# A hybrid decoder layer on one core: the order in which kept weight parts and output-projection operands are made, and which halves are scaled

## The chip, the core and the metric

The kernel runs on one core of a Trainium2 chip. A core has a matrix engine (TensorE, here PE, with its weight loads as PEld), a vector engine (VectorE, DVE), an activation engine (ScalarE, ACT), a general engine (GpSimd, POOL), a queue that here issues all DMAs (SyncE, SP), an on-chip memory, and PSUM banks into which PE writes. The metric is the device time of one execution in microseconds (us), lower is better.

## What is computed

One layer over 2048 tokens of width 1024, in fp32. The part that matters here, cut from the reference:

```python
u = rmsnorm(h, attn_pre_norm[i])
proj = u @ w_in[i]
hq, hf, hi, hg, sq, sk, sv = jnp.split(proj, splits, axis=-1)
o_hg = hgrn2_mix(hq, hf, hi, lb_all[i])
o_hg = rmsnorm(o_hg.astype(x.dtype), hg_out_norm[i]) * jax.nn.silu(hg)
o_sb = stick_breaking_mix(...)
o_sb = rmsnorm(o_sb, sb_out_norm[i])
mix = jnp.concatenate([o_hg, o_sb], axis=-1) @ w_out[i]
h = h + rmsnorm(mix, attn_post_norm[i])
u = rmsnorm(h, ffn_pre_norm[i])
gate, up = jnp.split(u @ w_gate_up[i], [D_FF], axis=-1)
y = (jax.nn.silu(gate) * up) @ w_down[i]
h = h + rmsnorm(y, ffn_post_norm[i])
h = h + (p[i] @ ple_proj[i]) * jax.nn.sigmoid(h @ ple_gate[i])
```

`rmsnorm` divides a row by the root of its mean square plus 1e-6 and multiplies by a gain.

## The kernel before

The 2048 tokens are four groups of 512 (`NG` groups, tiles of 128x512 throughout). Every fp32 product is made of three matmuls on rounded halves: an operand is cast to a high part by ACT, a low part is the difference, made by DVE or POOL (`split`, L203 to L207), and `mm3` (L218 to L221) multiplies high by high, high by low and low by high.

The first part of the program is a plan of input projections (`in_proj`): step by step a projection's matmuls are woven with units of attention, with steps of the HGRN recurrence (`hgrn`, 46 steps a group) and with other streams. `weave` (L51) runs a main stream slot by slot and gives each other stream its share of steps; `Rate` spreads a number of steps over a number of slots. Then come two plain output projections (groups 0 and 1, `out_proj`), with the rest of attention and HGRN woven in, and one joint output projection of groups 2 and 3 (`out_pair`). Joint projections, the FFN and the last gate use a seven-product scheme (`CHAIN = (1, 2, 6, 3, 7, 5, 4)`) instead of eight block products, whose operands are sums and differences of blocks. For the output projection and two blocks of the FFN, the weight operands of some products are made early, in spare time, split, and put away in DRAM: these are the kept parts. `out_combos` (L731) and `gate_up_combos` (L706) make them, `keep` (L700) casts, subtracts and stores one; `wo_p`, `wg_p` hold them.

What sets the order: PE runs in the order of the program text. On all other engines a planner reorders instructions by a simulated timeline: what is ready may go ahead of earlier text. `tc.keep_in_program_order` pins an instruction behind the instruction that was traced last before it on its engine; later instructions are not tied to it. All DMAs are issued by SP. A tile of a pool waits until one of the pool's buffers is free; the pool `xt` has 8 buffers and serves the kept parts, the operands of the output projections (`out_load`, L629) and the token tiles; the pool `u` holds 16 pairs of split operands.

Stages by the weight casts of L205 in an answer of the trace (24 to an attention-side projection, 32 to an HGRN-side one; the last two of the plan hold 2 and 4 of `out_load`):

| stretch, us | plan step | beside it |
| --- | --- | --- |
| 89 to 192 | 0, group 1, attention side | attention |
| 192 to 333 | 1, group 0, HGRN side | attention |
| 333 to 457 | 2, group 2, attention side | `out_combos` in the text |
| 457 to 626 | 3, group 1, HGRN side | attention, HGRN |
| 626 to 786 | 4, group 3, attention side | first half of `gate_up_combos` in the text |
| 786 to 963 | 5, group 2, HGRN side | its second half in the text |
| 963 to 1158 | 6, group 3, HGRN side | `out_load(0)` at once at its start |
| 1158 to 1256 | plain output projection 0 | `out_load(1)` at once at its start |
| 1256 to 1357 | plain output projection 1 | `first_rows`, `post_mix` of group 0 |

In the output projections the two halves of a row, HGRN and attention, have each their own mean square. In the plain ones the result of each half is scaled after the product. In the joint one, where blocks of both halves are added, each half was scaled before: `over_rows` (L769) spreads the factors of 512 rows over 128 partitions by four transposes on PE, and `scaled` (L779) multiplies; group 2 in `first_rows`, group 3 in the hook `before` (L852) at the second of the chain's 28 steps. The scaled tiles of group 2 go to DRAM (`on_s`) and are loaded again by `out_pair`. `post_mix` (L905) normalises a plain projection's result, adds the residual, transposes it and writes `h_s` and `u_s`; for group 1 its transposes are evicted (L930) into the pool `acc` of two buffers.

## Time and profile before

| | us |
| --- | --- |
| median of 3 runs | 3000.83 (2997.11 to 3003.03) |
| the profiled execution's own time | 2994.58 |
| its span, first to last instruction | 2992.7 |
| PE busy in it | 2869.8 |
| DVE busy | 2113.8 |
| ACT busy | 1579.3 |
| POOL busy | 1400.4 |

Busy time of one engine can be set beside the span: what is left is idle time of that engine. In a row of a table by stretches the columns are the stretch, its length, the busy time and number of instructions of PE, PEld, DVE, ACT and POOL, the share of the full clock that PE was granted, the busy share of the DMA engines and what they moved in GB/s. A group of instructions has its line, engine, operation, the tiles out<-in, shapes and count, then busy time in us, mean ns of one, idle time of the engine before them and what ended it. A wait's row has who waited, for what, then the us in total, the number of waits and the longest one. L1050, L1051, L1063 and L1066 are lines of helpers (`pair_of`, `sub`, `add`) that many callers share.

### The profile page before, as it was taken

Reading aid. Unit: us, or ns where it says so; the run is one execution under the profiler, and the core shown is the slowest. Engines: PE = TensorE matmul, PEld = TensorE weight load, DVE = VectorE, ACT = ScalarE, POOL = GpSimd, SP = SyncE. Lnnn points to the kernel's source line nnn. Section 1 sums busy time; section 2 is a strip of 40 time slices with the busy share of each in tenths; the row PEclk is TensorE's granted clock in tenths of the full one; section 3 lists DMA queues with packets and bytes.
Section 4 is the critical chain, followed back from the end, with each engine's and each line's share of the span. In section 5 each row is a group of like instructions: output and inputs, shape, how many; then the busy total and the mean of one; then the engine's idle time right before and its main releaser. Section 6 shows DMA issues by size and latency. Waiting matters only on the chain. (4 is left out here: it accounts for less than half of the span.)

```text
span 2992.7 us, 52029 instructions
## 1 busy us (share of the span) xinstructions
PE 2869.8 (96%) x17804; PEld 2402.7 (80%) x17804; DVE 2113.8 (71%) x3055; ACT 1579.3 (53%) x3222; POOL 1400.4 (47%) x1388
## 2 busy tenths in 40 slices
PE   8999999988999998988999999999999999999999
PEld 7888778877888787877787778788888888878777
DVE  4766776778777777667876777856777766666685
ACT  5676657666666666665633333455533333545542
POOL 3345446545555667665523222355822121456653
PEclk9999999999999999999999999999999999999999
DMA  7775685468545545358896687877975555667975
GB/s 226 234 200 164 208 278 169 142 197 262 166 144 150 145 131 163 110 161 297 310 304 210 225 292 259 267 216 221 311 238 172 176 169 176 214 213 233 332 251 169
DMA packets 488137, 636.32 MB, mean 213 GB/s; under 512 B 45248, under 2 KB 275648, under 8 KB 487872
## 3 DMA queue, kind: packets, MB, share of 16 engines
q1 hardware_dynamic: 487872, 633.00, 67.3%
q8 instruction: 141, 2.31, 0.3%
q14 instruction: 124, 1.02, 0.1%
HBM read 459.29 MB, written 173.54 MB: 211 GB/s over the span
## 5 line engine op out<-in xcount | busy, mean ns | idle before, releaser
L1050 ACT CAST wh<-wr 128x512 fp32r<-128x512 f32 x592 | 346.9, 618 | 498.0 <-PE mm L220 111.1
L1051 POOL TENSOR_TENSOR wl<-wr,wh 128x512 fp32r<-128x512 f32 x256 | 369.0, 1449 | 432.4 <-ACT wh L1050 383.9
L450 POOL TENSOR_TENSOR a<-be,ring 128x512 f32<-128x512 f32 (+2 forms) x320 | 328.1, 1025 | 425.3 <-DVE ring L446 387.1
L219 PE MATMUL mm<-uh,wh 128*128 128x512 f32 x968 | 403.7, 417 | 13.1 <-DVE eb L349 5.5
L1051 DVE TENSOR_TENSOR wl<-wr,wh 128x512 fp32r<-128x512 f32 x336 | 303.6, 911 | 158.5 <-ACT wh L1050 139.6
L220 PE MATMUL mm<-ul,wh 128*128 128x512 f32 x968 | 382.5, 395 | 0.0
L221 PE MATMUL mm<-uh,wl 128*128 128x512 f32 x968 | 382.5, 395 | 0.0
L446 DVE TENSOR_TENSOR_SCAN ring<-z,ring,be 128x512 f32<-128x512 f32 x192 | 245.5, 1279 | 101.1 <-ACT z L432 93.5
L219 PE MATMUL mm<-wh,uh 128*128 128x256 f32 (+1 forms) x840 | 260.8, 310 | 1.4 <-DVE eb L349 1.3
L220 PE MATMUL mm<-wl,uh 128*128 128x256 f32 (+1 forms) x840 | 247.2, 294 | 1.6 <-POOL wl L1051 1.6
L221 PE MATMUL mm<-wh,ul 128*128 128x256 f32 (+1 forms) x840 | 246.8, 294 | 0.0
L431 ACT ACTIVATE be<-z 128x512 f32<-128x512 f32 (+2 forms) x320 | 171.1, 535 | 100.9 <-DVE z L429 57.1
L219 PEld LDWEIGHTS mm<-uh,wh 128*128 128x128 f32 x968 | 184.9, 191 | 49.0 <-DVE eb L349 5.6
L463 DVE TENSOR_TENSOR al<-tr,ah 128x512 fp32r<-128x512 f32 (+1 forms) x320 | 191.2, 598 | 44.9 <-ACT ah L461 43.2
L221 PEld LDWEIGHTS mm<-uh,wl 128*128 128x128 f32 x968 | 183.9, 190 | 41.7
L205 ACT CAST wh<-wr 128x512 fp32r<-128x512 f32 x256 | 158.5, 619 | 106.6 <-PE mm L220 53.2
L461 ACT CAST ah<-tr 128x512 fp32r<-128x512 f32 (+1 forms) x320 | 167.7, 524 | 86.7 <-PE tr L458 85.0
L220 PEld LDWEIGHTS mm<-ul,wh 128*128 128x128 f32 x968 | 184.6, 191 | 30.8
L206 POOL TENSOR_TENSOR wl<-wr,wh 128x512 fp32r<-128x512 f32 x128 | 168.9, 1319 | 85.6 <-ACT wh L205 71.5
L458 PE MATMUL tr<-ident,a 128*128 128x128 f32 x1088 | 177.3, 275 | 25.6 <-POOL a L450 22.5
L1051 POOL TENSOR_TENSOR wl<-s,wh 128x512 fp32r<-128x512 f32 x40 | 65.7, 1644 | 268.1 <-ACT wh L1050 224.3
L425 PE MATMUL z<-kt,q 128*128 128x512 f32 (+3 forms) x640 | 189.0, 376 | 0.0
(387 smaller groups left out, 7616.3 us busy)
## 6 DMA issues: line engine op xcount, KB each, us to landing
wr<-in_w_gate_up_dram SPq DMA_DIRECT2D x292, 256.0 KB, 4.3
wr<-in_w_in_dram SPq DMA_DIRECT2D x224, 256.0 KB, 3.3
wr<-hid_s SPq DMA_DIRECT2D x154, 256.0 KB, 3.4
wr<-in_w_down_dram SPq DMA_DIRECT2D x110, 256.0 KB, 3.7
wr<-h_s SPq DMA_DIRECT2D x96, 256.0 KB, 4.6
wr<-wd_s SPq DMA_DIRECT2D x88, 256.0 KB, 3.2
kt<-k_s SPq DMA_DIRECT2D x80, 256.0 KB, 3.1
vt<-v_s SPq DMA_DIRECT2D x80, 256.0 KB, 3.2
```

Of the source, the lines that this page charges most:

```text
L206: (lo_engine or nc.gpsimd).tensor_tensor(lo, src, hi.bitcast(F32), op=ALU.subtract)
L219: nc.tensor.matmul(o, l[0], r[0], start=start, stop=False)
L220: nc.tensor.matmul(o, l[0], r[1], start=False, stop=False)
L221: nc.tensor.matmul(o, l[1], r[0], start=False, stop=stop)
L425: nc.tensor.matmul(z[:, :n], st["q"][i][:, tb * P:(tb + 1) * P], ch["k"][:, :n], start=i == 0, stop=i == 1)
L431: nc.scalar.activation(be[:, :n], z[:, :n], AF.Sigmoid, scale=0.125)
L446: nc.vector.tensor_tensor_scan(r[:, o:o + n][:, ::-1], z[:, :n][:, ::-1], be[:, :n][:, ::-1], init, op0=ALU.mult, op1=ALU.bypass)
L450: nc.gpsimd.tensor_tensor(a[:, :n], be[:, :n], r[:, o + 1:o + n + 1], op=ALU.mult)
L458: nc.tensor.transpose(tr[:, tb * P:(tb + 1) * P], ch["a"][tb][:, sb * P:(sb + 1) * P], ident)
L463: nc.vector.tensor_tensor(lo[:, lo_c:], tr[:, lo_c:], hi[:, lo_c:].bitcast(F32), op=ALU.subtract)
L1050: nc.scalar.copy(hi, src)
L1051: lo_engine.tensor_tensor(lo, src, hi.bitcast(F32), op=ALU.subtract)
```

## The change

- `split` takes a function for its cast; `out_load` yields after each operand and its casts are pinned. It runs as a stream: for group 0 along plan step 6, for group 1 along the first plain output projection.
- `keep`'s subtraction and the sums and differences of `gate_up_combos` and `out_combos` are pinned, with a yield after each. `out_combos` runs along plan steps 0 and 2 (14 steps each), `gate_up_combos` along 4 and 5 (16 each). Same operations, same data.
- In the joint projection only the attention halves are scaled, by the ratio of the two halves' factors (`ratio`); the HGRN halves are used as they are, and their factor is applied with the row scales after the product. `on_s` holds the attention half alone; the HGRN blocks are loaded from `o_s`. Subtractions of HGRN blocks move ahead of the chain, the hook moves from step 1 to step 3.
- In the plain projections attention's steps go into 24 slots instead of 27, HGRN's into 27 instead of 30; the streams of `first_rows` and `post_mix` are placed anew.
- HGRN's row sums use a bank of `tr` instead of `hg`, and the evictions of group 1's `post_mix` go to the pool `wr` (12 buffers) instead of `acc`.

```diff
@@ -121,7 +121,7 @@
     hid_s = [dram.tile([DFF // 256, 7, P, GT], F32, tag=f"hid_s{i}", name=f"hid_s{i}") for i in range(2)]
-    on_s = scratch("on_s", (ND, P, GT))
+    on_s = dram.tile([HH, P, GT], F32, tag="on_s", name="on_s")
     wo_s = [dram.tile([2, P, GT], F32, tag=f"wo_s{k}", name=f"wo_s{k}") for k in range(ND // 2)]
@@ -200,9 +200,11 @@
-    def split(pool, tag, bufs, src, lo_engine=None):
+    pin = tc.keep_in_program_order
+
+    def split(pool, tag, bufs, src, lo_engine=None, placed=lambda ins: ins):
         hi, lo = operand(pool, tag, bufs)
-        nc.scalar.copy(hi, src)
+        placed(nc.scalar.copy(hi, src))
         (lo_engine or nc.gpsimd).tensor_tensor(lo, src, hi.bitcast(F32), op=ALU.subtract)
@@ -627,26 +629,25 @@
     def out_load(g, res):
-        ops = []
-        acc = None
+        ops = res["o"] = []
         for i in range(ND):
...
                 gs = g_sb[:, i - HH:i - HH + 1]
-                nc.scalar.activation(hi, raw, AF.Copy, scale=gs)
+                pin(nc.scalar.activation(hi, raw, AF.Copy, scale=gs))
                 nc.vector.scalar_tensor_tensor(lo, raw, gs, hi.bitcast(F32), op0=ALU.mult, op1=ALU.subtract)
...
                 if i == HH:
-                    acc = ev(name="oss")
-                    nc.scalar.activation(acc, raw, AF.Square)
+                    res["oss"] = ev(name="oss")
+                    nc.scalar.activation(res["oss"], raw, AF.Square)
                 else:
                     nc.scalar.activation(raw, raw, AF.Square)
-                    nc.gpsimd.tensor_tensor(acc, acc, raw, op=ALU.add)
+                    nc.gpsimd.tensor_tensor(res["oss"], res["oss"], raw, op=ALU.add)
             else:
-                ops.append(split(wpool, "u", UB, raw))
-        res["o"], res["oss"] = ops, acc
+                ops.append(split(wpool, "u", UB, raw, placed=pin))
+            yield
@@ -699,7 +700,7 @@
         nc.scalar.copy(hi.bitcast(F32R), t)
-        nc.vector.tensor_tensor(lo.bitcast(F32R), t, hi, op=ALU.subtract)
+        pin(nc.vector.tensor_tensor(lo.bitcast(F32R), t, hi, op=ALU.subtract))
         for n, e in enumerate((hi, lo)):
@@ -716,16 +717,21 @@
                 a11, a12, a21, a22 = ts
-                add(V, a22, a21, a22)
-                sub(V, a21, a11, a21)
-                sub(V, a11, a22, a11)
-                sub(V, a12, a12, a11)
+                pin(add(V, a22, a21, a22))
+                yield
+                keep(wg_p[fb][n], 5, a22)
+                yield
+                pin(sub(V, a21, a11, a21))
+                yield
+                keep(wg_p[fb][n], 7, a21)
+                yield
+                pin(sub(V, a11, a22, a11))
                 yield
                 keep(wg_p[fb][n], 6, a11)
+                yield
+                pin(sub(V, a12, a12, a11))
+                yield
                 keep(wg_p[fb][n], 3, a12)
-                yield
-                keep(wg_p[fb][n], 7, a21)
-                keep(wg_p[fb][n], 5, a22)
                 yield
@@ -734,14 +740,22 @@
                 nc.sync.dma_start(t, w_out[r:r + P, n % 2 * GT:(n % 2 + 1) * GT])
-            keep(wo_p[k], 3, ts[3])
-            yield
-            b_combos(*ts, V)
-            nc.sync.dma_start(wo_s[k][0], ts[0])
-            nc.sync.dma_start(wo_s[k][1], ts[2])
-            keep(wo_p[k], 7, ts[1])
-            yield
-            keep(wo_p[k], 6, ts[3])
+            b11, b12, b21, b22 = ts
+            keep(wo_p[k], 3, b22)
+            yield
+            pin(sub(V, b11, b12, b11))
+            nc.sync.dma_start(wo_s[k][0], b11)
+            yield
+            pin(sub(V, b12, b22, b12))
+            yield
+            keep(wo_p[k], 7, b12)
+            yield
+            pin(sub(V, b22, b22, b11))
+            yield
+            keep(wo_p[k], 6, b22)
+            yield
+            pin(sub(V, b21, b22, b21))
+            nc.sync.dma_start(wo_s[k][1], b21)
             yield
@@ -762,10 +776,15 @@
-    def row_scale(rr):
-        nc.gpsimd.tensor_scalar(rr, rr, 1.0 / (HH * P), EPS, op0=ALU.mult, op1=ALU.add)
-        nc.gpsimd.tensor_tensor(rr, rr, neghalf.to_broadcast((P, TT)), op=ALU.pow)
-        return rr
+    def ratio(g, ss):
+        x = hgss[:, g, :]
+        for t in (x, ss):
+            nc.gpsimd.tensor_scalar(t, t, 1.0 / (HH * P), EPS, op0=ALU.mult, op1=ALU.add)
+        nc.gpsimd.tensor_tensor(ss, ss, neghalf.to_broadcast((P, TT)), op=ALU.pow)
+        nc.gpsimd.tensor_tensor(ss, ss, x, op=ALU.mult)
+        nc.gpsimd.tensor_tensor(x, x, neghalf.to_broadcast((P, TT)), op=ALU.pow)
+        nc.gpsimd.tensor_tensor(ss, ss, x, op=ALU.mult)
+        return ss
@@ -775,31 +794,31 @@
-    def scaled(g, i, raw, r):
-        if i < HH:
-            (nc.gpsimd if g == NG - 1 else nc.vector).tensor_tensor(raw, raw, r, op=ALU.mult)
-        else:
-            nc.vector.scalar_tensor_tensor(raw, raw, g_sb[:, i - HH:i - HH + 1], r, op0=ALU.mult, op1=ALU.mult)
-        if g == NG - 2:
-            nc.sync.dma_start(on_s[g][i], raw)
+    def scaled(k, raw, r):
+        nc.vector.scalar_tensor_tensor(raw, raw, g_sb[:, k:k + 1], r, op0=ALU.mult, op1=ALU.mult)
...
         yield
-        ss = tile_sums(acc)
-        rr = row_scale(hgss[:, g, :]), row_scale(ss)
+        r = ratio(g, tile_sums(acc))
         yield
-        for part in range(2):
-            r = over_rows(rr[part], "tr", xt)
-            yield
-            for k in range(HH):
-                raw = xt("raw")
-                nc.sync.dma_start(raw, o_s[g][part * HH + k])
-                scaled(g, part * HH + k, raw, r)
-                tt[1 + part, k] = split(wpool, "u", UB, raw, V if k % 2 else G)
-                if k % 2:
-                    yield
+        for k in range(HH):
+            raw = xt("raw")
+            nc.sync.dma_start(raw, o_s[g][k])
+            tt[1, k] = split(wpool, "u", UB, raw, V if k % 2 else G)
+            if k % 2:
+                yield
+        r = over_rows(r, "tr", xt)
+        yield
+        for k in range(HH):
+            raw = xt("raw")
+            nc.sync.dma_start(raw, o_s[g][HH + k])
+            scaled(k, raw, r)
+            nc.sync.dma_start(on_s[k], raw)
+            tt[2, k] = split(wpool, "u", UB, raw, V if k % 2 else G)
+            if k % 2:
+                yield
@@ -829,11 +848,11 @@
             if prod == 3:
-                a12 = load(on_s[g][HH + k])
+                a12 = load(on_s[k])
                 sub(V, s2[k], a12, s2[k])
...
             elif prod == 7:
-                t = load(on_s[g][k])
+                t = load(o_s[g][k])
                 sub(V, t, t, raws[k])
@@ -850,17 +869,12 @@
         def before(pos, i):
-            if (pos, i) == (0, 1):
-                raws["r"] = [over_rows(r, "tr", new_acc) for r in rr]
+            if (pos, i) == (0, 3):
+                r = over_rows(rr, "tr", new_acc)
                 for k in range(HH):
-                    scaled(g + 1, k, raws[k], raws["r"][0])
-                for k in range(HH):
-                    scaled(g + 1, HH + k, raws[HH + k], raws["r"][1])
-                    t = load(on_s[g][k])
-                    sub(V, t, raws[k], t)
-                    add(V, t, t, raws[HH + k])
-                    s2[k] = t
-                    tt[6, k] = split(wpool, "u", UB, t, V)
+                    scaled(k, raws[HH + k], r)
+                    add(V, s2[k], s2[k], raws[HH + k])
+                    tt[6, k] = split(wpool, "u", UB, s2[k], V)
@@ -874,6 +888,9 @@
             nc.sync.dma_start(raws[i], o_s[g + 1][i])
+        for k in range(HH):
+            s2[k] = load(o_s[g][k])
+            sub(V, s2[k], raws[k], s2[k])
         for k in range(HH):
@@ -898,8 +915,14 @@
                 half = 0 if prod == 5 else 1
-                for t in range(TT):
-                    row_rstd(None, rows_m[half][t], sums_m[half][:, 2 * t:2 * t + 2])
+                r, x = row_scales[:, half, 0:TT], hgss[:, g + half, :]
+                pair = sums_m[half].rearrange("p (t j) -> p t j", j=2)
+                nc.gpsimd.tensor_tensor(r, pair[:, :, 0], pair[:, :, 1], op=ALU.add)
+                for _ in range(2):
+                    nc.gpsimd.tensor_tensor(r, r, x, op=ALU.mult)
+                nc.gpsimd.tensor_scalar(r, r, EPS, None, op0=ALU.add)
+                nc.gpsimd.tensor_tensor(r, r, neghalf.to_broadcast((P, TT)), op=ALU.pow)
+                nc.gpsimd.tensor_tensor(r, r, x, op=ALU.mult)
@@ -1471,6 +1494,7 @@
     kept_out, kept_ffn = Stream(out_combos()), Stream(gate_up_combos())
+    loads = [Stream(out_load(g, res[g])) for g in range(2)]
     spent = 11
@@ -1484,14 +1508,14 @@
         toks = in_norm(nxt) if nxt else []
-        if n == 6:
-            out_load(0, res[0])
-        more = {2: kept_out, 4: kept_ffn, 5: kept_ffn}.get(n)
-        steps = {2: 3 * HH, 4: 6, 5: 6}.get(n)
-        more = Rate(more or idle, 1, steps or 0, slots - tail)
+        more, steps = {
+            0: (kept_out, 14), 2: (kept_out, 14), 4: (kept_ffn, 16), 5: (kept_ffn, 16), 6: (loads[0], ND)}.get(n, (idle, 0))
+        more = Rate(more, 1, steps, slots - tail)
         for r, c in zip(ra, cuts):
...
             weave(main, c, r.part(c), rh.part(c, 1 if hg_n < slots else None), more.part(c, 1))
+        if n in (2, 5, 6):
+            more.stream.drain()
         if n in (3, 5):
@@ -1501,9 +1525,9 @@
     todo = total_units - spent + LAG + 2
-    rates = Rate(att_stream, 2, todo, 2 * OP_SLOTS - 5)
+    rates = Rate(att_stream, 2, todo, 2 * OP_SLOTS - 8)
     r2 = Rate(hgs[2], 1, HG_STEPS - 42, 2)
-    r3 = Rate(hgs[3], 1, HG_STEPS, 2 * OP_SLOTS - 2)
+    r3 = Rate(hgs[3], 1, HG_STEPS, 2 * OP_SLOTS - 5)
     half = OP_SLOTS // 2
@@ -1517,22 +1541,25 @@
         if g == 0:
-            out_load(1, res[1])
             weave(op, 2, rates.part(2), r2.part(2))
             hgs[2].drain()
-            weave(op, OP_SLOTS - 2, rates.part(OP_SLOTS - 2), r3.part(OP_SLOTS - 2))
+            weave(op, OP_SLOTS - 2, rates.part(OP_SLOTS - 2), r3.part(OP_SLOTS - 2), (loads[1], ND, 0))
+            loads[1].drain()
         else:
             rows = Stream(first_rows(2, tto))
-            weave(op, 4, rates.part(4), r3.part(4), (pm, TT, 0), (rows, 2, 1))
+            weave(op, 4, rates.part(4), r3.part(4), (pm, TT, 0), (rows, 3, 1))
             weave(op, 2, rates.part(2), r3.part(2))
...
             square_sums(acc3, 0, 3, range(HH - 1), xt)
-            weave(op, 7, rates.part(7), r3.part(7), (pm, 2 * TT, 0), (rows, 5, 1))
+            weave(op, 2, rates.part(2), r3.part(2), (pm, TT // 2, 0))
             att_stream.drain()
             square_sums(acc3, 0, 3, (HH - 1,), xt)
-            weave(op, 3, r3.part(3), (rows, 2, 1))
+            weave(op, 3, r3.part(3), (pm, TT, 0), (rows, 1, 1))
+            ss3 = tile_sums(acc3)
+            weave(op, 2, r3.part(2), (pm, TT // 2, 0), (rows, 1, 1))
             hgs[3].drain()
-            rr3 = [row_scale(hgss[:, 3, :]), row_scale(tile_sums(acc3))]
+            rr3 = ratio(3, ss3)
+            weave(op, 3, (rows, 2, 1))
             rows.drain()
@@ -1544,7 +1571,7 @@
     op = Stream(out_pair(2, tto, rr3))
-    pm = Stream(post_mix(1, res[1]["mix"], ["tr", "hg", "tr"], lambda: slot("acc", 0, "acc")))
+    pm = Stream(post_mix(1, res[1]["mix"], ["tr", "hg", "tr"], lambda: slot("wr", 0, "wr")))
     def third_operands():
...
```

More of the change, by code (lines that the diff above doesn't have):

```diff
@@ L618, in hgrn @@
         yield
-        b = bank("hg")
+        b = bank("tr")
         for c in range(TT):
@@ L1062, in sub @@
     def sub(e, o, a, b):
-        e.tensor_tensor(o, a, b, op=ALU.subtract)
+        return e.tensor_tensor(o, a, b, op=ALU.subtract)
     def add(e, o, a, b):
-        e.tensor_tensor(o, a, b, op=ALU.add)
+        return e.tensor_tensor(o, a, b, op=ALU.add)
     V, G = nc.vector, nc.gpsimd
```

## The prediction

> **What bounds the kernel now.** I read the page first, then one table of busy times by stretches, cut where the changed work runs, then the waits inside those stretches.
>
> ```profile
> span 2992.7 us, 52029 instructions
> PE 2869.8 (96%) x17804; PEld 2402.7 (80%) x17804; DVE 2113.8 (71%) x3055; ACT 1579.3 (53%) x3222; POOL 1400.4 (47%) x1388
> ```
>
> TensorE (PE) is the bound. It lacks 2992.7 - 2869.8 = 122.9 us of being busy throughout, so a change that leaves its matmuls alone can win only from these idle times and from stretches in which its clock is not granted in full. The question is how much of both lies where this change works.
>
> ```profile
> core 0: us, PE busy (x) PEld busy (x) DVE busy (x) ACT busy (x) POOL busy (x), PEclk, DMA share, GB/s
> 91.00:190.00 99.00, 96.60 (x575) 83.67 (x574) 70.04 (x128) 63.90 (x143) 39.42 (x42) 1.00 0.77 220
> ...
> 336.00:424.00 88.00, 77.12 (x669) 63.52 (x667) 69.23 (x108) 49.08 (x99) 38.55 (x44) 0.94 0.85 274
> 424.00:629.00 205.00, 204.48 (x1732) 174.49 (x1731) 144.55 (x225) 143.34 (x316) 117.06 (x152) 1.00 0.58 168
> 629.00:724.00 95.00, 77.30 (x595) 61.98 (x594) 81.10 (x116) 59.49 (x122) 41.83 (x44) 0.93 0.76 235
> 724.00:788.00 64.00, 61.78 (x551) 51.76 (x551) 48.26 (x75) 42.27 (x96) 39.09 (x49) 1.00 0.66 204
> 788.00:960.00 172.00, 170.75 (x1403) 145.35 (x1403) 131.17 (x188) 117.82 (x247) 97.56 (x125) 1.00 0.50 149
> 960.00:1000.00 40.00, 35.78 (x331) 28.71 (x330) 32.03 (x43) 28.46 (x58) 30.75 (x30) 1.00 0.54 161
> 1000.00:1160.00 160.00, 155.84 (x1536) 130.41 (x1535) 116.92 (x178) 108.97 (x232) 99.76 (x122) 1.00 0.49 141
> 1160.00:1200.00 40.00, 33.73 (x323) 29.68 (x322) 26.35 (x39) 26.26 (x53) 29.76 (x38) 1.00 0.53 161
> 1200.00:1297.00 97.00, 88.46 (x1067) 80.17 (x1066) 66.08 (x110) 59.02 (x135) 65.49 (x80) 0.95 0.42 127
> 1297.00:1377.00 80.00, 66.30 (x736) 61.25 (x735) 46.25 (x77) 50.06 (x126) 47.55 (x54) 0.98 0.62 197
> 1377.00:1442.00 65.00, 54.70 (x243) 44.54 (x242) 55.50 (x77) 42.82 (x104) 31.91 (x25) 0.92 0.85 299
> 1442.00:2993.00 1551.00, 1521.62 (x6756) 1250.83 (x6754) 1088.40 (x1463) 633.83 (x1179) 615.59 (x454) 0.99 0.73 236
> ```
>
> Idle is a row's length minus its PE busy time. It is 10.9 us in 336:424 and 17.7 in 629:724, but only 0.5 in the 205 us between them and 1.3 in 788:960. The granted clock dips in the same two rows: (1 - 0.94) x 88 = 5.3 us and (1 - 0.93) x 95 = 6.7 us of full clock are missing, partly while PE idled anyway. What runs there and nowhere else is the making of kept weight parts:
>
> ```profile
> L702 DVE TENSOR_TENSOR kl<-wg,kh x16: 658/680/1578, 646.0 to 718.5; 128x512 fp32r<-128x512 f32 x16
> L702 DVE TENSOR_TENSOR kl<-wo,kh x12: 660/678/1582, 350.5 to 418.0; 128x512 fp32r<-128x512 f32 x12
> ```
>
> The program traces these over a whole input projection (`out_combos`) or two (`gate_up_combos`), but the planner lets them float forward: all 28 ran in two bursts of some 70 us. The waits (us in total, times, longest) name the link. In 336:424 PE's longest wait is for an eviction on VectorE (DVE):
>
> ```profile
> PE mm L219 <- DVE eb L349: 6.8, 3, 5.5
> ```
>
> In 629:724 it is for an attention weight of POOL, and POOL itself waited there for the scan on DVE:
>
> ```profile
> PE tr L458 <- POOL a L450: 12.5, 5, 4.7
> ```
>
> ```profile
> POOL a L450 <- DVE ring L446: 29.9, 16, 6.5
> ```
>
> Evictions and scans are DVE work, queued among the burst's.
>
> **The change part by part.**
>
> *Kept parts.* The DVE work that is moved, in 336:424
>
> ```profile
> L1063 DVE TENSOR_TENSOR wo<-wo 128x512 f32<-128x512 f32 x16 | 13.9, 869 | 5.8 <-DMA wo<-in_w_out_dram 3.8 <-issue 2.0
> L702 DVE TENSOR_TENSOR kl<-wo,kh 128x512 fp32r<-128x512 f32 x12 | 9.6, 800 | 0.4 <-DMA wo_s<-wo 0.4
> ```
>
> and in 629:724
>
> ```profile
> L702 DVE TENSOR_TENSOR kl<-wg,kh 128x512 fp32r<-128x512 f32 x16 | 14.0, 887 | 1.2 <-DMA wg_p<-kh 1.2
> L1063 DVE TENSOR_TENSOR wg<-wg 128x512 f32<-128x512 f32 x12 | 9.7, 811 | 0.0
> L1066 DVE TENSOR_TENSOR wg<-wg 128x512 f32<-128x512 f32 x4 | 3.6, 903 | 3.5 <-DMA wg<-in_w_gate_up_dram 3.4
> ```
>
> That is 13.9 + 9.6 = 23.5 us of DVE in 88 us, and 14.0 + 9.7 + 3.6 = 27.3 us in 95. A pin puts each behind the DVE instruction traced before it, so it cannot float forward. Half of the first work goes to 91:190, the rest stays in 336:460; the second spreads over 629:960. Nothing is saved on DVE; the density falls from about 27% of DVE's time to 8 to 12%. What stays of the idle (late next in the first stretch is PE itself, in the second the scan's own chain) I take from the nearest row without a burst, 724:788: 2.2 / 64 = 0.035 us per us. First stretch: 10.9 - 3 = 7.9 us won; second: 17.7 - 3.3 = 14.4. Of the clock I count two thirds: 3.5 + 4.4. Together 30.2. Bounds: at most 28.6 + 12 = 40.6, at least nothing. Where the work lands it costs something: DVE is busy 70.04 / 99 = 71% in 91:190 and 76% in 788:960. I charge 6 us, between nothing (those rows idle 2.4 and 1.3 us) and 22 (all of the excess idle moves along). The casts of the parts move along on ScalarE (ACT), one of some 0.6 us for each `kl`, 17 us in all on an engine that is 53% busy; they are not pinned. The DMAs move along on SP: 24 of the first set's 48 transfers of 128x512 fp32 enter 91:190, 6.3 MB or 64 GB/s on 220, little more than the 274 that 336:424 carried, and below the rate of 1377:1442. Net 24.
>
> A rule speaks against the spreading. The Trainium skill, "SBUF — State Buffer", section "SBUF: two separate sides", says that a DVE operation with two SBUF inputs and a GpSimd operation that reads SBUF exclude each other for a whole instruction. The trace agrees: the same subtraction took 658 ns at least and 1578 at most. By the rule 788:960, where POOL is busy 97.56 / 172 = 57% instead of 44%, makes moved operations dearer: 32 x 13% x 0.92 us, an estimated 4 us of DVE at most, and the sum would be 35 were all of that PE's.
>
> *Operand loads, `out_load`.* The same happens to the eight operands of each plain output projection:
>
> ```profile
> L634 SPq DMA_DIRECT2D raw<-o_s x16: 319/420/893, 722.7 to 990.6; - x16
> L638 ACT ACTIVATE uh<-raw,g_sb x8: 710/723/742, 970.7 to 1174.7; 128x512 fp32r<-128x512 f32 x8
> ```
>
> They are cast right at the start of the stage whose finished operands free the buffers, near 960 and 1160. Those two 40 us rows idle 4.2 and 6.3 us, against 4.2 in the 160 us between. Spread, they would keep 1 each; I take half of the rest, 4, and charge 1: 3 us. Bounds 0 and 8.
>
> *Plain output projections, 1200:1377.* Attention's steps go into 24 slots instead of 27, HGRN's into 27 instead of 30. Same work, denser early, none in the last three slots. Waits of 1160:1377:
>
> ```profile
> PE hg L604 <- DVE sl L600: 11.2, 5, 4.8
> PE hg L540 <- POOL qp L577: 8.6, 4, 3.2
> ```
>
> These belong to HGRN's own chain (mask level, POOL product, next level) and remain. The attention squares, with their loads and sums, no longer come last. I take a gain of 2; bounds: 14 gained (half of 8.5 + 13.7 idle and 6.5 clock), 19 lost (rival 2).
>
> *Joint projection, 1377:1442.* Idle 10.3, clock (1 - 0.92) x 65 = 5.2. PE's waits, then one of SP's queue, then what kept POOL:
>
> ```profile
> PE tr L926 <- ACT acc L930: 5.5, 1, 5.5
> PE z L220 <- DMA ul<-wo_p: 4.0, 1, 4.0
> ```
>
> ```profile
> SPq L917 <- POOL h L916: 5.1, 1, 5.1
> ```
>
> ```profile
> 1392.22 2.68 SPq L917 DMA_DIRECT2D h_s<-h  x2
> 1394.99 1.35 SPq L818 DMA_DIRECT2D uh<-wo_p  x3
> ```
>
> ```profile
> L780 POOL TENSOR_TENSOR wr<-wr,acc x2: 1409/1574/1739, 1385.5 to 1386.8; 128x512 f32<-128x512 f32 x2
> ```
>
> The 4.0 us for `wo_p`: its loads stood on SP behind a store that waited 5.1 us for POOL's L916, and POOL was on the row scalings of the HGRN halves, four in all and at the median of these two 4 x 1.57 = 6.3 us. The change removes these four, moves four subtractions ahead, and needs one broadcast instead of two. The 5.5 us waits for an eviction into one of two `acc` buffers; it now goes to a `wr` buffer, of which there are 12. Against it, the hook of product 6 comes two steps later: 24 matmuls x 54.70 / 243 us = 5.4 us, and the whole of it could come back as a new wait. I take 9 of 15.5; bounds -5 and 15.5. The extra POOL work (`ratio`, six operations for four; `rows_m`, six for eight) is on 128x4 columns off the chain. Eight broadcast transposes of 17804 PE instructions go; at PE's mean of 2869.8 / 17804 = 0.16 us that is an estimated 1.3, taken as 1. The 1551 us after 1442 run the same program: 0.
>
> **Sum:** 24 + 3 + 2 + 9 + 1 = 39 us. The profiled execution took 2994.58 us (span 2992.7 and 1.9 around it), 6.25 below the runs' median of 3000.83. 2994.58 - 39 = 2955.6; on the median's footing 3000.83 - 39 = 2961.8, so **2962**.
>
> **Rivals.**
>
> 1. *The stalls spread with the work.* Each us of moved DVE work idles PE as in the burst: the 22 us come back, instead of 6, and half of the 7.9 clock with them. 39 - 16 - 4 = 19: **2982**. For it: DVE is above 70% busy in every row that receives work, and the port conflict above. Against: 788:960 idles 1.3 us at 76%.
>
> 2. *HGRN stands bare.* Attention ends in slot 8 of the second projection, and five slots of denser HGRN have little cover. 1297:1377 is such a stretch today (13.7 idle). Twice as much is 14 more. Short gaps cost clock too:
>
> ```profile
> 1219.00:1232.00 13.00, 11.16 (x106) 10.53 (x105) 6.70 (x13) 5.52 (x12) 7.10 (x12) 0.87 0.40 122
> 1225.21 0.54 PE L604 MATMUL hg<-score,v 128*128 128x128 f32 x2 [1.84 <-DVE sl L600]
> ```
>
> Around a gap of 1.84 us 0.13 x 13 = 1.7 us of clock are missing. Three such dips make the loss 19: 39 - 2 - 19 = 18, **2983**. By the Trainium skill, "TensorE: Matmul & The Clock Gate", section "HAM oscillation — how this bites in real kernels", only idle gaps over about 3.4 us bite, so the dips would not come (2978); this row differs.
>
> 3. *It doesn't do what it says.* A pin is only a lower bound on the place; planner and buffers may bunch the work again, and other waits take the freed time: **3000**.
>
> 4. *Slower: a pinned operation waits at the head of its queue.* Eight groups' first operations and the 16 casts of `out_load` hang on a DMA; those from and to `raw` landed after
>
> ```profile
> DMA to landing us min/median/max: 2.0/3.9/6.9
> ```
>
> Behind a pinned one that is late stand scans and evictions, and behind them PE. All 24 at the median cost 94 us. From (39 + 6) / 24 = 1.9 us each the result is slower; at 2.2 it is 39 - 53 = -14: **3015**. Against: loads aren't pinned and can run ahead (the first raws were issued at 722.7, and casts of them still ran at 970.7), and today's waits of the 16 `wo` subtractions for their loads sum to 3.8 us.
>
> **How the numbers follow.** Forecast 0.61, rivals 0.12, 0.10, 0.08 and 0.09 in this order. Faster by over 0.2% (6 us, about what a measurement of this kernel can tell from no change): 0.61 + 0.12 + 0.10 = 0.83; within 0.2%: 0.08; slower: 0.09. Low end: the upper bounds of the kept parts (40.6 without charge), of 1377:1442 (15.5) and half of the others' (7): 63, so 2938. High end: the forecast with the joint projection at its worst (9 + 5 lost) and rival 2's 21, 2962 + 35 = 2997, so 2996; rivals 3 and 4 lie outside.
>
> **What would show it.** Right: the `kl` rows span 91 to 460 and 629 to 960; PE idle in the two burst stretches falls from 28.6 to some 7, with clock 0.98 or more; PE's waits for `eb` and `a` there shrink; no wait for `wo_p` in the joint projection and none of 5 us at L926. Wrong: PE idle that appears in 91:190 and 788:960 in the same amount; DVE or ACT idle at L702, L1063 or L638 until a DMA; longer `sl` and `qp` waits; a new wait of product 6 for DVE's `ul`.

## The result, and the profile after

The changed kernel takes 2968.42 us (median of 4 runs, 2960.92 to 2975.07); the kernel before took 3001.93 beside it (4 runs, 2997.11 to 3005.14). The ratio is 0.9889, 95% interval 0.9861 to 0.9917: 33.5 us by the medians, where 39 were forecast. The profiled execution took 2966.78 us, 27.8 less than that of before.

The head of the page after:

```profile
span 2965.0 us, 51986 instructions
PE 2862.4 (97%) x17796; PEld 2397.8 (81%) x17796; DVE 2114.2 (71%) x3051; ACT 1581.2 (53%) x3220; POOL 1387.7 (47%) x1384
```

PE is not busy for 2965.0 - 2862.4 = 102.6 us, 20.3 less than before. The other 7.4 us of the span are PE busy time, which holds the eight transposes and the time at a lower clock. DVE has as much work as before.

The table by stretches after, cut at the stages of the changed kernel (rows as before):

```profile
core 0: us, PE busy (x) PEld busy (x) DVE busy (x) ACT busy (x) POOL busy (x), PEclk, DMA share, GB/s
90.00:201.00 111.00, 100.29 (x587) 86.27 (x585) 81.66 (x140) 66.96 (x150) 42.80 (x43) 0.98 0.79 232
...
342.00:453.00 111.00, 109.01 (x1003) 91.28 (x1002) 83.41 (x134) 68.17 (x144) 56.64 (x63) 1.00 0.71 211
453.00:622.00 169.00, 168.47 (x1401) 144.53 (x1400) 119.15 (x185) 121.55 (x265) 97.52 (x133) 1.00 0.57 172
622.00:767.00 145.00, 136.07 (x1142) 113.07 (x1141) 115.96 (x175) 96.79 (x207) 76.10 (x92) 0.98 0.62 183
767.00:944.00 177.00, 175.32 (x1432) 149.18 (x1430) 146.83 (x208) 124.70 (x259) 106.16 (x128) 1.00 0.61 185
...
1349.00:1420.00 71.00, 58.99 (x244) 46.07 (x244) 50.35 (x74) 45.66 (x110) 26.32 (x23) 0.90 0.86 299
1420.00:2965.00 1545.00, 1518.83 (x6755) 1249.49 (x6753) 1095.51 (x1468) 635.41 (x1179) 609.64 (x449) 1.00 0.73 237
```

Plan step 2 (342:453) idles 2.0 us, step 4 (622:767) 8.9, step 5 (767:944) 1.7. Step 0 (90:201) idles 10.7 us, where before 91:190 idled 2.4. The joint projection (1349:1420) idles 12.0 us, against 10.3 before, in a stretch 6 us longer.

To set stages beside each other I counted the split-product matmuls (those of `mm3`: 10968 in either kernel) from the start, and took the time at which the same one begins in both traces. A stage's entry is the time it took in that kernel minus the time it took before, so a negative entry is a gain (profiled executions; "again" is the changed kernel profiled a second time, as experiment e9):

| stage (times of before) | forecast | after | again |
| --- | --- | --- | --- |
| to 91 | 0 | -1.7 | -0.8 |
| step 0, 91 to 194 | part of +6 | +10.7 | +7.2 |
| steps 1 and 3 | 0 | -0.3 | -0.2 |
| step 2, 335 to 460 | -11.4 | -13.5 | -13.1 |
| step 4, 629 to 789 | -18.8 | -14.8 | -16.0 |
| step 5, 789 to 966 | part of +6 | +0.7 | +0.6 |
| step 6, 966 to 1161 | half of -3 | +0.9 | -0.7 |
| plain output projections, 1161 to 1378 | -2, half of -3 | -7.7 | -3.8 |
| joint: "first product", 1378 to 1389 | part of -9 | +8.8 | +8.9 |
| joint: the rest, to 1442 | part of -9 | -5.2 | -5.7 |
| after 1442 | 0 | -5.7 | -14.9 |
| span | -39 | -27.7 | -38.4 |

(The forecast's 1 us for the transposes stands in no single row.) The row "first product" is a short name: by the matmuls the joint projection begins at 1374.2 before and at 1347.2 after, with the first step of its first product, which the table counts with the plain projections; the row runs from the second step of that product to the end of the first step of the second product. From its own first matmul to 1442 the joint projection loses 4.9 us (4.4 again), and the plain ones win 8.9 (5.0).

The last stage runs the same program, and one kernel differs there by 9.2 us from one execution to the next, with its waits at different places. That is the error of a comparison of two traces, so I take the stages that repeat, and the medians for the whole. Up to 1442, where the changed work runs, the two traces win 22.0 and 23.6 us.

The changed kernel's kept parts, by tile (columns: min/median/max ns, first and last start):

```profile
L703 DVE TENSOR_TENSOR kl<-wg,kh x16: 677/954/1801, 647.9 to 952.9; 128x512 fp32r<-128x512 f32 x16
...
L703 DVE TENSOR_TENSOR kl<-wo,kh x12: 666/684/1484, 102.8 to 455.8; 128x512 fp32r<-128x512 f32 x12
```

The two bursts are gone. PE's waits (us in all, times, longest) in step 2 and in step 4 after:

```profile
PE mm L221 <- DVE eb L351: 1.2, 1, 1.2
```

```profile
PE tr L460 <- POOL a L452: 8.4, 8, 3.0
```

Over the same two stages before, the waits for `eb` and `a` were 6.8 and 14.7 us, and there was one of 3.3 for `vv` (12.5 of the 14.7 stood in the burst's stretch). The same view of step 0, before and then after, shows what came in there:

```profile
PE tr L458 <- POOL a L450: 1.4, 2, 0.8
PE mm L219 <- DVE vv L363: 0.8, 1, 0.8
```

```profile
PE tr L460 <- POOL a L452: 4.4, 6, 1.2
PE mm L221 <- DVE vv L365: 3.6, 1, 3.6
PE mm L221 <- DVE eb L351: 2.7, 3, 1.6
```

The longest of these can be followed link by link. First ACT's timeline after (start, length; in brackets the idle time before it and what ended that), then DVE's, then PE's:

```profile
153.76 0.62 ACT L702 CAST kh<-wo 128x512 fp32r<-128x512 f32 x1 [2.93 <-DMA wo<-in_w_out_dram]
154.28 0.37 ACT L364 CAST vv<-mm 128x256 fp32r<-128x256 f32 x1
```

```profile
154.68 0.42 DVE L365 TENSOR_TENSOR vv<-mm,vv 128x256 fp32r<-128x256 f32 x1 [2.54 <-ACT vv L364]
```

```profile
156.38 0.47 PE L221 MATMUL mm<-uh,wh 128*128 128x512 f32 x1 [3.64 <-DVE vv L365]
```

The cast of a kept part stands at the head of ACT's queue until its load lands; an eviction is queued behind it; DVE waits for that, and PE for both. It is the mechanism of rival 4, on an instruction that the change does not pin. In the second profile this wait for `vv` is 1.6 us, and step 0 loses 7.2 instead of 10.7.

PE's waits in the joint projection after:

```profile
PE av L222 <- DVE wl L846: 5.8, 1, 5.8
PE z L223 <- DVE ul L208: 3.2, 2, 2.7
PE mm L222 <- DVE ul L846: 1.5, 1, 1.5
PE z L221 <- ACT uh L207: 1.0, 1, 1.0
PE z L222 <- DMA ul<-wo_p: 0.3, 1, 0.3
```

The wait for `wo_p` (4.0 us) is nearly gone and so are the 5.5 us at `post_mix`'s transposes. In their place stands one of 5.8 us, for the low part of the second product's last weight block. Its load, on SP's timeline, and its subtraction, on DVE's:

```profile
1355.62 0.83 SPq L842 DMA_DIRECT2D wr<-in_w_out_dram  x1
```

```profile
1361.03 0.75 DVE L798 SCALAR_TENSOR_TENSOR wl<-wl,g_sb,acc 128x512 f32<-128x512 f32 x1 [6.71 <-ACT acc L794]
...
1369.95 0.68 DVE L846 TENSOR_TENSOR wl<-wr,wh 128x512 fp32r<-128x512 f32 x1
```

That load goes out at 1355.6, some 8 us after the joint projection's first matmul (1347.2). ACT casts the block at 1363.7 to 1364.4, and DVE comes to its low part 5.6 us later: the operations of the hook and others stand before it. By tile `wr`, before (the loads' first and last start are the last two times):

```profile
L823 SPq DMA_DIRECT2D wr<-in_w_out_dram x8: 327/330/426, 1342.0 to 1369.1; - x8
```

There the last of them went out 5.1 us ahead of the first matmul (1374.2).

### The profile page after: what moved, and what is told of

It is laid out like the page before. It is cut to its first block, busy times and chain, and to the rows that moved or that the text cites. A ratio compares the mean times of both kernels' runs of the same rounds, so it can differ in the third digit from the quotient of the medians.

```text
span 2965.0 us, 51986 instructions
## 1 busy us (share of the span) xinstructions
PE 2862.4 (97%) x17796; PEld 2397.8 (81%) x17796; DVE 2114.2 (71%) x3051; ACT 1581.2 (53%) x3220; POOL 1387.7 (47%) x1384
```

## The experiments

Every ratio is to the kernel before, run beside it on the same chip, with its 95% interval. Three sets of runs were made, each on one chip: e1 to e4, e5 to e8, e9 to e12. Stage entries are made as in the table above.

**e1, the kept parts alone.** The kernel before, with the change's `keep`, `out_combos`, `gate_up_combos` and their places in the plan, and nothing else of it:

```diff
...
-        more = {2: kept_out, 4: kept_ffn, 5: kept_ffn}.get(n)
-        steps = {2: 3 * HH, 4: 6, 5: 6}.get(n)
+        more, steps = {
+            0: (kept_out, 14), 2: (kept_out, 14), 4: (kept_ffn, 16), 5: (kept_ffn, 16)}.get(n, (idle, 0))
```

> Kernel before, with the kept parts alone as in the change: a yield and a pin for each operation, the first set along plan steps 0 and 2, the second along 4 and 5; operand loads, plain and joint projections as before. If the kept parts carry the win (the prediction's first term; the stages of the changed kernel's trace give +10.7 us in step 0, -13.5 in step 2, -14.8 in step 4, +0.7 in step 5), the time is 15 to 20 us under the kernel before. If the win needs the operand loads or the pacing of the projections as well, it is under 8.

Measured: 2977.62 against 2993.85, ratio 0.9950 (0.9935 to 0.9965): 16 us, as expected. Steps 2 and 4 win 12.8 and 16.0, step 0 loses 7.4, and a loss stands in step 6: 6.8. There, the tiles named `raw` tell why. Their loads begin at 944.6 in e1, and at 722.7 in the row of before that the prediction quotes:

```profile
L636 SPq DMA_DIRECT2D raw<-o_s x16: 319/350/577, 944.6 to 971.0; - x16
```

The pool `xt` is now held by kept parts to the end of step 5 (the last `kl` of e1 starts at 948.6), so `out_load` cannot run ahead, and traced at once its operands arrive in a bunch where step 6 begins. What it costs there, in e1:

```profile
PE hg L542 <- POOL ring L442: 3.8, 1, 3.8
```

```profile
944.00:984.00 40.00, 33.54 (x290) 26.14 (x289) 28.54 (x38) 25.99 (x53) 28.37 (x28) 0.87 0.59 189
```

PE waits for a product of HGRN on POOL (`qp`, done at 973.2, just before the small operation that the row names). POOL had run without a break since 962.0, and three of its operations there are sums of squares of these operands. Besides, 0.13 x 40 = 5.2 us of full clock are missing; in the same stretch of e6, below, PE idles 1.3 us at the full clock. In e12 the last `kl` starts at 925.7, the loads of `raw` at 927.4, some 17 us ahead of step 6, and step 6 loses nothing (-0.1).

**e2, the same without pins.** As e1, with one line changed:

```diff
-    pin = tc.keep_in_program_order
+    pin = lambda ins: ins
```

> The same with the yields and the plan steps of the kept parts, but no pin. If the pins hold the work back (theory), the subtractions run forward in bursts again and 10 us or more of the win are lost. If the finer steps and the new places alone do it (rival: a pin is only a lower bound that seldom binds), the time is within 3 us of e1.

Measured: 2995.31, ratio 1.0004 (0.9991 to 1.0016): no difference in the whole. By tile in e2:

```profile
L704 DVE TENSOR_TENSOR kl<-wg,kh x16: 656/674/1579, 649.4 to 712.5; 128x512 fp32r<-128x512 f32 x16
...
L704 DVE TENSOR_TENSOR kl<-wo,kh x12: 667/684/1576, 96.9 to 380.1; 128x512 fp32r<-128x512 f32 x12
```

The weights for the FFN are again made within 63 us, though the text spreads them over two projections; the stretch of that burst in e2:

```profile
633.00:727.00 94.00, 77.40 (x579) 62.27 (x578) 77.25 (x114) 57.73 (x118) 41.98 (x42) 0.89 0.74 237
```

It idles 16.6 us, and step 4 wins nothing (+1.9, in an execution of 3004.05 us, the longest of ten). So the text does not spread this work until it is pinned, and the burst is what costs. The text does move the output projection's parts to step 0, and there they cost without a pin too: step 0 loses 9.1, step 2 wins 5.1.

**e12, pins alone.** The kernel before with the same DVE operations pinned, its old yields and its old steps:

```diff
-                add(V, a22, a21, a22)
-                sub(V, a21, a11, a21)
...
+                pin(add(V, a22, a21, a22))
+                pin(sub(V, a21, a11, a21))
```

> Kernel before with the pins on the kept parts' subtractions and sums alone: their steps, groups of operations and plan steps as before. If the pins carry the win of the kept parts, the low parts spread over plan steps 2, 4 and 5 and it is 10 to 17 us faster than before, like e1. If an operation at a time is needed as well (rival), groups of four to six still stand in front of evictions, and it wins less than 8.

Measured: 2969.74 against 2994.56, ratio 0.9926 (0.9911 to 0.9940), 25 us, more than the 10 to 17 expected. By tile in e12:

```profile
L704 DVE TENSOR_TENSOR kl<-wg,kh x16: 659/761/1779, 667.4 to 925.7; 128x512 fp32r<-128x512 f32 x16
...
L704 DVE TENSOR_TENSOR kl<-wo,kh x12: 674/688/1781, 348.9 to 456.9; 128x512 fp32r<-128x512 f32 x12
```

Step 0 keeps its time, step 2 wins 7.6, step 4 wins 17.8, step 5 loses 4.3. Against e1, "one operation at a time" brings some 4 in step 5; in step 2, where e1 has only half of the work, it is e3 below that can be compared, with 10.5 against 7.6. The changed kernel itself, run beside e12 as e9, wins 29 us, 4.5 more, and the intervals overlap (0.9886 to 0.9916 for e9). Up to 1442 the trace of e12 wins 21.8 us, about as much as the changed kernel's (22.0 and 23.6). What all the other edits of the changed kernel bring together, beyond the pins and with step 0's loss among them, is not shown to be more than nothing.

**e3, no kept parts in step 0.** The changed kernel, with all 28 steps of `out_combos` along step 2:

```diff
-            0: (kept_out, 14), 2: (kept_out, 14), 4: (kept_ffn, 16), 5: (kept_ffn, 16), 6: (loads[0], ND)}.get(n, (idle, 0))
+            2: (kept_out, 28), 4: (kept_ffn, 16), 5: (kept_ffn, 16), 6: (loads[0], ND)}.get(n, (idle, 0))
```

> Changed kernel, with all 28 steps of the output projection's kept parts in plan step 2 and none in step 0. If step 0 lost its 10.7 us to these operations (theory: PE waits behind an ACT cast that waits for its load, and behind DVE), it comes back within 2 us of the kernel before there, step 2 gives up 2 to 6 us, and the whole is 5 to 8 us faster than the changed kernel. Rival: twice the density in step 2 brings the waits back there, and the whole is the same as the changed kernel or slower.

Measured: 2960.98, ratio 0.9893 (0.9877 to 0.9909). Steps 0 and 2 in e3:

```profile
91.00:194.00 103.00, 100.62 (x609) 87.71 (x608) 72.71 (x134) 65.60 (x149) 41.76 (x44) 1.00 0.77 221
...
335.00:450.00 115.00, 110.67 (x1019) 92.56 (x1018) 94.15 (x148) 72.48 (x154) 59.93 (x65) 1.00 0.84 260
```

Step 0 has its time of before, and step 2 still wins 10.5, with DVE busy 82%. By stages that is 4 to 8 us better than the changed kernel, as expected; the whole cannot be told from it by these intervals.

**e11, step 0's operations on POOL.** The changed kernel, with the differences and low parts of the first two `out_combos` groups on POOL:

```diff
+            e = G if k < 2 else V
-            keep(wo_p[k], 3, b22)
+            keep(wo_p[k], 3, b22, e)
...
-            pin(sub(V, b11, b12, b11))
+            pin(sub(e, b11, b12, b11))
```

> Changed kernel, with the sums and low parts of the output projection's kept parts in plan step 0 on POOL, not VectorE. If step 0 loses its 8 to 11 us because evictions stand behind these on VectorE (theory), 5 us or more of it come back. Rival: it loses them to the ACT casts that stand until their weights have landed and to the added transfers; then it stays above 7 us.

Measured: 2961.47, ratio 0.9891 (0.9872 to 0.9909); step 0 loses 5.7, against 7.2 in e9 beside it. PE's waits in step 0 of e11:

```profile
PE mm L221 <- DVE vv L365: 4.3, 1, 4.3
PE tr L460 <- POOL a L452: 2.0, 3, 0.8
```

With DVE relieved, the waits for `a` fall (4.4 to 2.0) and those for `eb` (2.7) are gone, but the wait behind ACT's cast is longer (in e9 it was 1.6), so only 1.5 us come back, fewer than expected. DVE's load is a part of step 0's price; the stall behind loads is another. How much of the 7 to 11 us is due to each stays open.

**e6, kept parts and operand loads.** e1, with `out_load` as a pinned stream along step 6 and the first plain projection, as in the change:

```diff
-        if n == 6:
-            out_load(0, res[0])
...
+            0: (kept_out, 14), 2: (kept_out, 14), 4: (kept_ffn, 16), 5: (kept_ffn, 16), 6: (loads[0], ND)}.get(n, (idle, 0))
```

> Kernel e1 with the operand loads as streams, as in the change; pacing and joint projection as before. e1 lost 6.8 us in plan step 6 against the kernel before. If that is the burst of operand loads, which can no longer run ahead since the kept parts hold the buffers (theory), step 6 comes back to within 2 us of before, and the whole is 5 to 8 us faster than e1. Rival: step 6 lost it to something else and stays.

Measured: 2975.36 against 2999.02, ratio 0.9921 (0.9896 to 0.9947), 24 us. Step 6 goes from 6.8 lost (e1) to 0.7 won. The stream mends what the kept parts in e1 broke; that step is then no faster than before. (e6, e7 and e11 have two runs each.)

**e7, the old pacing.** The changed kernel, with attention's and HGRN's steps of the plain projections in 27 and 30 slots as before, and the streams of `first_rows` and `post_mix` beside them near their old places:

```diff
-    rates = Rate(att_stream, 2, todo, 2 * OP_SLOTS - 8)
+    rates = Rate(att_stream, 2, todo, 2 * OP_SLOTS - 5)
...
-    r3 = Rate(hgs[3], 1, HG_STEPS, 2 * OP_SLOTS - 5)
+    r3 = Rate(hgs[3], 1, HG_STEPS, 2 * OP_SLOTS - 2)
...
```

> Changed kernel, with attention over 27 slots and the recurrence over 30, as before, and the smaller streams of the second plain projection near their old places. If the pacing gave the 9 us that the changed kernel won in the last part of that projection (theory), they go: 5 to 10 us slower than the changed kernel. Rival: the ratio, with its half of the row scalings gone, gave them; then no change over 2 us.

Measured: 2963.57, ratio 0.9882 (0.9857 to 0.9908). The loss expected from the old pacing did not come. From 1161 to 1442 (times of before) e7 takes 275.3 us, the changed kernel 275.6 and 279.0, e6 284.4, before 279.6. PE's waits around the end of the second projection in e7:

```profile
PE hg L606 <- DVE sl L602: 4.9, 1, 4.9
PE z L221 <- DMA uh<-wo_p: 2.4, 1, 2.4
PE z L222 <- DMA ul<-wo_p: 1.7, 2, 0.9
```

HGRN's wait at the end is back, but the 5.8 us for `wl` is gone and the first product loses 0.4 instead of 8.8. Its weight loads, of which the last goes out 4.9 us ahead of the first matmul (1349.3):

```profile
L842 SPq DMA_DIRECT2D wr<-in_w_out_dram x7: 327/345/385, 1324.9 to 1344.4; - x7
```

So the denser pacing takes the idle time from the end of the second plain projection and puts it into the first product of the joint one; its net is nothing that these runs can tell. Scaling the attention halves only, with what else differs between e6 and e7 (the place of the streams and the `wr` evictions), comes to 284.4 - 275.3 = 9 us here, by one trace of each; half of it pays back what e6 lost there against the kernel before (284.4 - 279.6 = 4.8).

**e4 and e5, what holds that last weight load?** e4 traces the weights of the second product ahead of the four loads and subtractions of HGRN blocks; e5 puts the hook of product 6 back to step 1. Both are edits of the changed kernel:

```diff
+        for k in range(HH):
+            w_prep(1, k)
         for k in range(HH):
             s2[k] = load(o_s[g][k])
             sub(V, s2[k], raws[k], s2[k])
-        for k in range(HH):
-            w_prep(1, k)
```

> Changed kernel, with the loads and subtractions of the HGRN blocks behind the weights of the chain's second product in the text, not ahead of them. If the 5.8 us wait for the low part of such a weight at the end of the first product comes from that order (theory), it goes, and the first product, now 8.8 us longer than before, is within 3 us of before; the whole is 4 to 8 us faster than the changed kernel. Rival: the wait comes from the hook's bunch of DVE work, which stays: no change over 2 us.

```diff
-            if (pos, i) == (0, 3):
+            if (pos, i) == (0, 1):
```

> Changed kernel, with the hook of product 6 back at the chain's second step, from the fourth. If the first product's 8.8 us come from VectorE standing at the hook's first scaling (idle 6.7 us until the broadcast is there) with the low part of a weight behind it (theory), the hook done 5 us earlier takes most of the 5.8 us wait away: the first product is within 3 us of before, the whole 5 to 9 us faster than the changed kernel. Rival: the late load of that weight alone holds it; then no change over 2 us.

Both miss. e4: 2967.74, ratio 0.9919 (0.9902 to 0.9935); the wait is 5.8 us as in the changed kernel and the last load goes out at 1356.3. e5: 2965.38, ratio 0.9885 (0.9864 to 0.9906); in its profiled execution, the longest of its five with 2983.75 us, the first product loses 12.9 instead of 8.8, the last load goes out at 1357.4, and its waits are now two:

```profile
PE av L221 <- ACT wh L845: 5.8, 1, 5.8
PE av L222 <- DVE wl L846: 3.5, 1, 3.5
```

Neither the order of the text nor the hook is what makes the load late; the pacing does, together with the places of the streams that e7 moves along with it. Whether a buffer or the queue on SP carries it was not tried.

**e8, e9 and e10, is there a better version?** e8 joins e3 and e5; e10 joins e3 and e7; e9 is the changed kernel itself, on the chip of e10.

> Changed kernel with both: the output projection's kept parts in plan step 2 alone, and the hook at the chain's second step. If e3's stage win (about 8 us) and e5's add, 12 to 16 us faster than the changed kernel, a ratio of about 0.985 to the kernel before. If e5 brings nothing, as e3, 0.989.

> The changed kernel itself, beside the other three of this set on one chip: a ratio of 0.989 to the kernel before, and the same stages within 2 us: +8 to +11 us in plan step 0, -13 to -15 in steps 2 and 4, +9 in the first product of the joint projection.

> Changed kernel with the output projection's kept parts in plan step 2 alone (as e3) and the old pacing (as e7). If the new pacing only moves idle time from the end of the second plain projection to the first product of the joint one (theory), plan step 6 to the end of the joint projection takes as long as in the changed kernel within 2 us, the wait for the weight's low part is gone, that for HGRN's last state is back; and with step 0 relieved the whole is 6 to 9 us faster than the changed kernel, about 0.986. Rival: the pacing is worth its 9 us; then the whole is no faster than the changed kernel.

| | median, us | before beside it | ratio (95%) |
| --- | --- | --- | --- |
| e8 | 2960.36 | 2999.02 | 0.9870 (0.9847 to 0.9893) |
| e9 | 2965.23 | 2994.56 | 0.9901 (0.9886 to 0.9916) |
| e10 | 2960.08 | 2994.56 | 0.9888 (0.9875 to 0.9900) |

e9 repeats the result. In e8 step 0 keeps its time, and the first product loses 10.2 us. e10 has neither step 0's loss (0.0) nor the first product's (0.4), which were 16 us in e9; but in return it wins 0.2 instead of 5.3 in the second plain projection, where its wait for `sl` is 7.0 us, 1.9 instead of 5.7 in the rest of the joint one, and 10.9 instead of 13.1 in step 2. 5 us remain by the medians, fewer than expected, and the intervals overlap: no version here is shown to beat the changed kernel. Pins alone are beaten: e10 is 9.7 us faster than e12 beside it (2960.08 and 2969.74), and these two intervals do not overlap. So the other edits bring something once no work lands in step 0.

## Why the prediction was right, and which sizes were off

The forecast of 2962 lies 6.4 us below the measured median, and the direction and its main mechanism hold. How near the number came is in part luck: up to 1442, where the forecast put all of its 39 us, the two traces win 22.0 and 23.6, and they win the rest after 1442, where the forecast put nothing. Point by point:

- **The burst is what cost, and the pin removes it.** Right, and shown both ways: without pins nothing is won (e2), pins alone win 25 us (e12). The 30.2 us priced for the two stretches measured 28.3 and 29.1; with steps 0 and 5 the term's 24 us net measured 16.9 and 21.3. The `kl` rows span 102.8 to 455.8 and 647.9 to 952.9, as forecast. In step 4 the scan's chain still makes PE wait 8.4 us for `a`, where 3.3 us of idle were to stay besides the 2.2 of 724:788; in step 2 the win was larger than priced.
- **The charge of 6 us for where the work lands** was mis-sized, and misplaced. It fell on step 0 almost alone: 10.7 and 7.2 us, and 0 in e3 and e12 where nothing lands there. Step 5, with DVE busier (146.83 of 177 us, 83%, after), took its half for 0.7. I had judged by the busy share of DVE, and that does not tell the two apart. In step 0 PE waits for evictions, for attention's operations and behind a cast whose load is late; why step 5 has so little of this stays open.
- **Operand loads: 3 won, measured about 0.** The term took the loads' own idle time for the gain. It did not ask what the kept parts, spread to the end of step 5, do to the pool that the loads share: without the stream they cost 6.8 us there (e1). The edit is worth some 7 us beside kept parts that last to the end of step 5, and nothing shows a gain beside those of e12, which end earlier. No run has it alone.
- **Plain projections: 2 won, measured 7.7 and 3.8; joint projection: 9 won, measured 3.6 and 3.2 lost.** Together 11 were forecast, without the operand loads' share, and 4.1 and 0.6 measured. The causes removed were the right ones (no wait for `wo_p` beyond 0.3, none at the transposes of `post_mix`), but I priced the stretches apart. I had put the danger at product 6, whose operands the hook makes; the new wait came earlier, in the first step of the second product, for a weight block whose load the denser pacing leaves too late.
- **The 1551 us after 1442: 0.** The two profiles of the changed kernel win 5.7 and 14.9 there. e1 and e12, which do not touch the joint projection, win some 3 to 4; e2 and e6 nothing. The variants of the changed kernel run from 10.7 won (e4) to 8.0 lost (e5). With this spread no gain of the change is shown.
- **Rivals.** The first (stalls spread in proportion) is refuted by step 5 and, with all the work left in step 2, by e3; in step 0 it came true, with 7 to 11 us lost for half of the first set. The second (HGRN bare) did not come: PE's waits between 1141 and 1349 after, below, hold none over 3.0 us, where one for `sl` cost 4.8 before. The third (the change does not bind) is near to what happens without pins, and e2 gives its time, 1.0004. The fourth was a mechanism that is there, at a smaller size: one cast in step 0 waits 2.93 us for its load, not 24 operations 2 us each.

```profile
PE hg L553 <- POOL qp L579: 6.1, 4, 2.3
PE hg L542 <- POOL qp L579: 3.9, 5, 1.5
PE hg L542 <- DVE ks L581: 3.9, 2, 2.2
PE hg L586 <- ACT score L573: 3.0, 1, 3.0
```

- **The low end of the range** takes half of the plain projections' bound alone as "half of the others'" (7); with the operand loads' bound of 8 it would be 11, and the low end 2934.
- **Dearer subtractions** came as the prediction allowed. The `kl` of the FFN weights rose from a median of 680 to 954 ns, spread over steps 4 and 5, where POOL is busy 76.10 / 145 = 52% and 106.16 / 177 = 60%; the burst ran beside a POOL busy 44%. By the medians that is 16 x 0.27 = 4.4 us of DVE. POOL's share is not the whole of it: over the same steps in e12 the median is 761. Of the 28 `kl` after, the 14 that took 801 ns or more all began while a POOL operation was running, and of the 14 that took 687 ns or less two did. The rule of the Trainium skill that speaks of this, "SBUF — State Buffer", section "SBUF: two separate sides" (a DVE operation with two SBUF inputs and a GpSimd operation that reads SBUF exclude each other), agrees with it. PE did not pay: step 5 lost 0.7 us.

## What to carry to other kernels

Work in spare time that a planner may move forward ran here as a burst, and the burst, on the engine that also evicts, stopped TensorE; bind the place of such work, and see by the first and last start that it holds. Try that alone first: here the pins by themselves won 25 us, and the whole change 29 beside them. Choose the stage that takes the work by trying: where DVE was 71% busy it cost 7 to 11 us, where it was 76% busy it cost 0.7, so ask who is queued behind the new work and its loads. When an earlier stage is packed closer, look for the first thing that the next stage can no longer have ready; a gain counted in one stretch alone may only be moved.

## What the runs showed of the hardware that I had not expected

A short gap can cost more than itself. Around a gap of 3.03 us in step 4, from 755.1 to 761.9, the granted clock was 0.50. The two rows are PE's timeline and a stretch around it, after:

```profile
755.95 0.47 PE L460 MATMUL tr<-ident,a 128*128 128x128 f32 x1 [3.03 <-POOL a L452]
```

```profile
750.00:765.00 15.00, 11.97 (x79) 10.50 (x78) 9.40 (x13) 8.39 (x21) 7.32 (x9) 0.77 0.58 176
```

0.23 x 15 = 3.4 us of full clock are missing there, more than the gap. By the Trainium skill, "TensorE: Matmul & The Clock Gate", section "HAM oscillation — how this bites in real kernels", a gap of that length would not bite; this row differs. The price is not fixed. The same gap of 3.03 us in e9 cost half of that:

```profile
750.00:765.00 15.00, 11.97 (x83) 10.93 (x82) 9.38 (x13) 8.14 (x19) 7.51 (x10) 0.89 0.58 173
```

Around one of 2.82 us in the kernel before (at 708.11) the clock was 1.00 from 704 to 717.

Also, one program's last 1550 us differed by 9.2 us between two executions (1544.9 and 1535.7 in the changed kernel), a third of the effect under study. This row of e9 stands against 1420:2965 above:

```profile
1419.00:2954.00 1535.00, 1513.38 (x6752) 1247.80 (x6750) 1090.01 (x1467) 635.98 (x1178) 613.00 (x449) 1.00 0.73 238
```
